# A hybrid decoder step on one core: the input moved ahead of the memory projections, attention keys loaded in 32-channel blocks and transposed by VectorE

## The chip, the core and the metric

The kernel runs on one core of a Trainium2 chip. The metric is the device time of one execution in microseconds (us). TensorE (PE) multiplies, VectorE (DVE) and ScalarE (ACT) do the elementwise work, GpSimd (POOL) does little here, and SyncE (SP) issues most of the DMA transfers. SBUF is the on-chip memory of 128 partitions; PSUM is where PE writes.

## What is computed

One layer of a decoder, for a prompt of 256 tokens and for 8 sample sequences of 4 tokens that share the weights; the two are put side by side as 288 columns. All data are float32.

```python
def mem_kv(mem, g_mem, w_k, w_v):
    m = rms_norm(mem, g_mem)                      # 256 memory tokens x 2048
    k = (m @ w_k).reshape(B, M, X_HEADS, X_HEAD_DIM)   # 4 heads of 512
    v = (m @ w_v).reshape(B, M, X_HEADS, X_HEAD_DIM)
...
def cross_attn(h, k, v, w_q, w_o):
    q = (h @ w_q).reshape(B, S, X_HEADS, X_HEAD_DIM)
    s = einsum('bqhd,bkhd->bhqk', q, k) * (X_HEAD_DIM ** -0.5)
    pr = softmax(s, axis=-1)
    return einsum('bhqk,bkhd->bqhd', pr, v).reshape(B, S, D_MODEL) @ w_o
...
    h = rms_norm(x, g_mix)
    z = h @ w_in                                  # 2048 x 11264: u, v, conv, pool, gates
    ...                                           # three branches, gates, merged
    x = x + merged @ w_out
    x = x + cross_attn(rms_norm(x, g_xattn), mk, mv, w_xq, w_xo)
    x = x + square(relu(rms_norm(x, g_mlp) @ w_up)) @ w_down
```

For the prompt, `mk` and `mv` are `mem_kv` of `mem_prompt` and are outputs too. For the samples they are read from `cache_mem_k` and `cache_mem_v`, 8 batches of 256 tokens by 4 heads by 512 channels: 4 x 512 KB of keys and as much of values for each batch.

## The kernel before, in words

**Weights.** Every product streams its weight matrix from DRAM in chunks of 512 rows by 512 columns (1 MB, four tiles of 128 rows). A list, `plan`, holds the order of the chunks. `load_w` issues a chunk's load on SP's queue into one of three buffers `raw` (L151). `split_w` makes of each half chunk (two tiles, 128 partitions x 1024) a high part on ACT (L165, `w_hi`) and a low part on DVE (L166, `w_lo`); a half is split two halves ahead of its use (`AHEAD`). Activations are split in the same way (`split_act`, `gain_hi`, `gain_lo`, L186 to L193).

**Products.** `proj` keeps the weights stationary and moves 288 columns of activations: for each tile and each of four groups of 128 output channels three matmuls, L232 to L234. `proj_mem`, for the two memory projections, keeps the 256 memory tokens stationary and moves 512 columns of the weights, for each tile and each group of 128 tokens three matmuls, L267 to L269: a half chunk is 12 of them.

**Side work.** `later(n, fn)` puts a function on a list; after each half chunk `tick` runs what is due (in `proj_mem` half a step after each tile). So everything that is not a product is placed by a number of half chunks, and stands in the engines' queues between two products.

**Order before.** The memory rows `mem_prompt` come first (four loads `mem_p`), are transposed by PE (`mem_first`, L348) and projected with `w_xk`, four heads one after the other, while x is loaded (L428 and the line before it), transposed (L434, L435) and normed behind the products. Then `w_in` and the branches, `w_branch`, `w_out`, and `w_xq`. During the last quarter of `w_xq` the memory rows are loaded a second time (`mraw`, L882) and transposed again (`mem_again`), and `w_xv` follows. The samples' attention runs beside `w_xv`: 16 units of 128 memory tokens of a batch, each one 1 MB load of 128 partitions (`k_load`, L901), 16 transposes by PE (L912) that go through PSUM to `kT` by one copy on ACT and one on DVE (L913) for each four, and 16 matmuls of 128 columns (`k_scores`, L921). A unit is due every 0.7 half chunks. `sample_softmax` (L932 to L939), `sample_probs` and 16 units of values (`sample_values`, L969) follow. The prompt's own keys are read back from `k_scr`, head by head (`head_load`, L989), transposed by PE (`head_keys`, L1002) and multiplied (L1011 to L1013, L1032 to L1034). `w_xo` and the MLP end the kernel.

Of the kernel before, what the change touches and what calls it, by code (L numbers as in the profile page):

```python
# [16 lines left out]
P = 128  # L17
# [21 lines left out]
def decoder_step_kernel(  # L39
# [41 lines left out]
    gmem = const.tile([P, 16], F32, name="gmem")  # L81

# [3 lines left out]
    # ---- work that is issued a number of weight steps later, between the products  # L86
# [28 lines left out]
    # ---- operands: weights streamed and split into high and low parts, activations kept split  # L115
# [5 lines left out]
    for h in range(4):  # L121
        planned(w_xk, KT, h * 512)
# [34 lines left out]
    def split_w(i):  # L157
        raw = raws[i // 2]
        t0 = 2 * (i % 2)
        hi = wpool.tile([P, 2, 512], F32R, name="w_hi", tag="w_hi")  # L160
        lo = wpool.tile([P, 2, 512], F32R, name="w_lo", tag="w_lo")
        n = 1 if i == 0 else 2
        for t in range(0, 2, n):
            src = raw[:, t0 + t:t0 + t + n]
            latest["hi"] = s_.copy(hi[:, t:t + n], src)  # L165
            latest["lo"] = v_.tensor_tensor(lo[:, t:t + n], src, hi[:, t:t + n].bitcast(F32), ALU.subtract)  # L166
        halves[i] = (hi, lo)
        if i % 2:
            del raws[i // 2]
# [29 lines left out]
    class Quarters:  # L199
        """Split activations, four channel tiles to a buffer."""  # L200
# [73 lines left out]
    # ---- norms  # L274
# [54 lines left out]
    def rows_rstd(pieces, rows, r_out):  # L329
        ss = small.tile([P, 4], F32, name="ss")  # L330
        n = 0
        for piece in pieces:
            width = min(1024, piece.shape[-1])
            for o in range(0, piece.shape[-1], width):
                junk = actp.tile([P, 1024], F32, name="junk", tag="q_lo3")
                s_.activation(junk[:rows, :width], piece[:rows, o:o + width], AF.Square,
                              accum_out=ss[:rows, n:n + 1])
                n += 1
        ms = small.tile([P, 1], F32, name="ms1")
        v_.reduce_sum(ms[:rows], ss[:rows, :n], axis=AX.X)  # L340
        v_.tensor_scalar(ms[:rows], ms[:rows], 1.0 / DM, RMS_EPS, ALU.mult, ALU.add)
        rpow(r_out, ms[:rows])

    def mem_transposed(nat, m, k2, k0=0):
        pt = psum()
        for d in range(2):
            for c in range(2):
                t_.transpose(pt[:, d * 256 + c * P:d * 256 + (c + 1) * P],  # L348
                             nat[c][:, (k2 - k0 + d) * P:(k2 - k0 + d + 1) * P], ident)
        for part in (gain_hi, gain_lo):  # L350
            for d in range(2):
                part(m.hi(k2 + d), m.lo(k2 + d), pt[:, d * 256:(d + 1) * 256], gmem[:, k2 + d:k2 + d + 1])

    # ------------------------------------------------------------------ branch phase
# [27 lines left out]
    v_.tensor_copy(gmem, vt[:, :16])  # L382
# [5 lines left out]
    later(6, load_vecs)  # L388

    class Halves:  # L390
        def hi(self, kt):
            return mh[kt // 8][:, kt % 8, :]

        def lo(self, kt):
            return ml[kt // 8][:, kt % 8, :]

    mh = [bp.tile([P, 8, MEM], F32R, name=f"mh{i}", tag=("u", "cv")[i]) for i in range(2)]
    ml = [bp.tile([P, 8, MEM], F32R, name=f"ml{i}", tag=("yh", "yl")[i]) for i in range(2)]
    m0 = Halves()

    def mem_first(k2):
        mem_transposed([mem_p[k2 // 4][:, c, :] for c in range(2)], m0, k2, k2 // 4 * 4)
    mem_first(0)
    with tc.issue_after(latest["a_hi"].ins), tc.issue_after(latest["a_lo"].ins):
        advance(0 - AHEAD)
    mem_first(2)
    for i in range(6):
        later(i + 1, lambda i=i: mem_first(4 + 2 * i))
    for c in range(2):
        later(3 + c, lambda c=c: rows_rstd([mp_[:, c, :] for mp_ in mem_p], P, r_mem[:, c:c + 1]))  # L410

    # x: transposed, kept for the residual, normed
    xbox = {}
    x_natp = bp.tile([P, 2, DM], F32, name="x_natp", tag="m")
    xT0 = actp.tile([P, KT, NT], F32, name="xT0", tag="xT")
    r_x = small.tile([P, 3], F32, name="r_x")

    x_nats = []

    def load_x():  # L420
        for c in range(2):
            nc.sync.dma_start(x_natp[:, c, :], x_prompt[0, c * P:(c + 1) * P, :])

    def load_xs():
        xs_ = x_sample.rearrange("b q d -> (b q) d")
        for i in range(2):
            xn = sig([P, 1024], f"x_nats{i}")
# [784 lines left out]
```

## Time and profile before

| what | value |
|---|---|
| time, median of 3 runs | 2191.64 us (2190.96 to 2195.14) |
| span of the profiled execution | 2190.5 us |
| PE busy | 2167.8 us, 99% of the span |
| DVE busy | 1258.6 us, 57% |
| ACT busy | 883.9 us, 40% |
| granted TensorE clock, mean | 0.999 of full speed |
| DMA | 399.63 MB, 182 GB/s over the span |

The runs' times lie around the profiled span; the median is 1.1 us above it. Busy time of PE is modelled from pipelined matmuls, so the distance from one start to the next is the better measure of what an instruction costs there.

### The profile page before, as it was taken

How to read it: one execution, taken by the hardware profiler on the slowest of the kernel's cores; microseconds unless marked ns; L12 is line 12 of the kernel's file. 1: busy time of each engine (PE TensorE's matmuls, PEld its weight loads, DVE VectorE, ACT ScalarE, POOL GpSimd, SP SyncE). 2: the span in 40 equal slices, each digit the busy share in tenths (PEclk: the TensorE clock that was granted, in tenths of full speed). 3: DMA queues.
4: the chain of work that ended last, by engine and by line, in shares of the span. 5: the costliest groups of instructions: out<-in, count | busy, mean ns of one | idle time of the engine just before them, and what ended most of it. 6: DMA issues, size and time to landing. Idle time of an engine off the chain costs nothing.

```text
span 2190.5 us, 37794 instructions
## 1 busy us (share of the span) xinstructions
PE 2167.8 (99%) x16134; PEld 2095.5 (96%) x16134; DVE 1258.6 (57%) x1909; ACT 883.9 (40%) x1200; POOL 27.2 (1%) x72
## 2 busy tenths in 40 slices
PE   8999999999999999999999999999999999999998
PEld 6799999999999999999887799999999999999998
DVE  4656678766775746464555556554455445445554
ACT  6533444333433544343443444333333333333343
POOL 1000000000000000000000000000000000000000
PEclk9999999999999999999999999999999999999999
DMA  8765554455454455444778745555554455555542
GB/s 297 243 202 166 191 176 155 137 172 169 159 173 159 165 203 192 163 165 161 245 277 304 283 164 164 161 167 172 158 171 163 165 170 159 173 162 166 173 155 101
DMA packets 185355, 399.63 MB, mean 182 GB/s; under 512 B 7130, under 2 KB 8778, under 8 KB 180555
## 3 DMA queue, kind: packets, MB, share of 16 engines
q1 hardware_dynamic: 180229, 386.45, 53.3%
q10 hardware_dynamic: 4702, 10.72, 1.3%
q8 instruction: 126, 2.06, 0.4%
q14 instruction: 42, 0.34, 0.0%
q0 software_dynamic: 256, 0.05, 0.0%
HBM read 385.60 MB, written 12.80 MB: 182 GB/s over the span
## 4 chain that ended last, share of the span: by engine, by line
PE 60%; issue 37%; DMA 1%; DVE 1%; ACT 0%; POOL 0%; SPq 0%; POOLq 0%; ACTq 0%; DVEq 0%
PE ps L232 15%; PE ps L234 15%; PE ps L233 15%; PE ps L267 3%; PE ps L268 3%; PE ps L269 3%; PE ps L912 1%; PE ps L921 1%; PE ps L969 1%; DMA kv<-in_cache_mem_v_dram 0%; DMA mem_p<-in_mem_prompt_dram 0%; DMA kv<-in_cache_mem_k_dram 0%; PE ps L683 0%; PE ps L348 0%; PE ps L434 0%
## 5 line engine op out<-in xcount | busy, mean ns | idle before, releaser
L166 DVE TENSOR_TENSOR w_lo<-raw,w_hi 128x1024 fp32r<-128x1024 f32 (+1 forms) x641 | 783.5, 1223 | 821.5 <-ACT w_hi L165 818.7
L165 ACT CAST w_hi<-raw 128x1024 fp32r<-128x1024 f32 (+1 forms) x641 | 670.8, 1047 | 1131.0 <-PE ps L233 987.8
L232 PE MATMUL ps<-q_hi,w_hi 128*128 128x288 f32 x3200 | 945.9, 296 | 0.0
L234 PE MATMUL ps<-q_hi,w_lo 128*128 128x288 f32 x3200 | 943.8, 295 | 0.9 <-DVE w_lo L166 0.9
L233 PE MATMUL ps<-q_lo,w_hi 128*128 128x288 f32 x3200 | 942.2, 294 | 0.0
L232 PEld LDWEIGHTS ps<-q_hi,w_hi 128*128 128x128 f32 x3200 | 600.4, 188 | 1.1
L234 PEld LDWEIGHTS ps<-q_hi,w_lo 128*128 128x128 f32 x3200 | 600.2, 188 | 1.1 <-DVE w_lo L166 1.1
L233 PEld LDWEIGHTS ps<-q_lo,w_hi 128*128 128x128 f32 x3200 | 600.3, 188 | 0.5
L232 PE MATMUL ps<-h_hi,w_hi 128*128 128x288 f32 x1024 | 303.5, 296 | 0.0
L233 PE MATMUL ps<-h_lo,w_hi 128*128 128x288 f32 x1024 | 302.8, 296 | 0.0
L234 PE MATMUL ps<-h_hi,w_lo 128*128 128x288 f32 x1024 | 300.9, 294 | 0.0
L234 PEld LDWEIGHTS ps<-h_hi,w_lo 128*128 128x128 f32 x1024 | 192.6, 188 | 0.0
L233 PEld LDWEIGHTS ps<-h_lo,w_hi 128*128 128x128 f32 x1024 | 192.3, 188 | 0.0
L232 PEld LDWEIGHTS ps<-h_hi,w_hi 128*128 128x128 f32 x1024 | 192.2, 188 | 0.0
L232 PE MATMUL ps<-y_hi,w_hi 128*128 128x288 f32 x384 | 113.6, 296 | 0.0
L233 PE MATMUL ps<-y_lo,w_hi 128*128 128x288 f32 x384 | 113.4, 295 | 0.0
L234 PE MATMUL ps<-y_hi,w_lo 128*128 128x288 f32 x384 | 112.9, 294 | 0.0
L568 DVE SCALAR_TENSOR_TENSOR cv<-glu,cwT,cv 128x256 f32<-128x256 f32 x240 | 105.7, 477 | 0.0
L234 PEld LDWEIGHTS ps<-y_hi,w_lo 128*128 128x128 f32 x384 | 72.2, 188 | 0.0
L232 PEld LDWEIGHTS ps<-y_hi,w_hi 128*128 128x128 f32 x384 | 72.0, 188 | 0.0
L233 PEld LDWEIGHTS ps<-y_lo,w_hi 128*128 128x128 f32 x384 | 72.1, 188 | 0.0
L267 PE MATMUL ps<-w_hi,mh 128*128 128x512 f32 x128 | 52.5, 418 | 0.9 <-ACT w_hi L165 0.9
(305 smaller groups left out, 1437.5 us busy)
## 6 DMA issues: line engine op xcount, KB each, us to landing
raw<-in_w_in_dram SPq DMA_DIRECT2D x88, 1024.0 KB
raw<-in_w_up_dram SPq DMA_DIRECT2D x64, 1024.0 KB
raw<-in_w_down_dram SPq DMA_DIRECT2D x64, 1024.0 KB
raw<-in_w_branch_dram SPq DMA_DIRECT2D x24, 1024.0 KB
raw<-in_w_out_dram SPq DMA_DIRECT2D x16, 1024.0 KB
kv<-in_cache_mem_k_dram SPq DMA_DIRECT2D x16, 1024.0 KB
raw<-in_w_xq_dram SPq DMA_DIRECT2D x16, 1024.0 KB
raw<-in_w_xv_dram SPq DMA_DIRECT2D x16, 1024.0 KB
```

What stands on the lines that cost most here:

```text
L165: latest["hi"] = s_.copy(hi[:, t:t + n], src)
L166: latest["lo"] = v_.tensor_tensor(lo[:, t:t + n], src, hi[:, t:t + n].bitcast(F32), ALU.subtract)
L232: t_.matmul(o, wh, act.hi(kt), start=kt == 0, stop=False)
L233: t_.matmul(o, wh, act.lo(kt), start=False, stop=False)
L234: t_.matmul(o, wl, act.hi(kt), start=False, stop=kt == nkt - 1)
L267: t_.matmul(acc[c], mh, hi[:, i, :], start=kt == 0, stop=False)
L268: t_.matmul(acc[c], mh, lo[:, i, :], start=False, stop=False)
L269: t_.matmul(acc[c], ml, hi[:, i, :], start=False, stop=kt == KT - 1)
L568: v_.scalar_tensor_tensor(o, i, wk, o, ALU.mult, ALU.add)
L912: t_.transpose(pt[:, i * P:(i + 1) * P], kv[:, kt * P:(kt + 1) * P], ident)
L921: t_.matmul(ssc[32 * h:32 * h + 32, c * P:(c + 1) * P], qm[:, 4 * h + k, b, :], kTs[h // 2][:, (h % 2) * 4 + k, :], start=b == 0 and c == ...
L969: t_.matmul(sbox["osc"][32 * h:32 * h + 32, :], sbox["pTm"][:, c, b, h, :], kv[:, h * 512:(h + 1) * 512], start=b == 0 and c == 0, stop=b ...
```

## The change

x and the first chunks of `w_in` are loaded first, with a gain column of their own (`gx`). `x_first` transposes x, splits x times gain without the norm and keeps x; the first group of `w_in` (columns 2048 to 2559) is multiplied with that, and the norm `rb` is applied when its sums leave PSUM. Behind it `x_normed` overwrites the activations with the normed ones for the other groups. The side work of this part is due some seven half chunks later.

`mem_prompt` is loaded once, in the last quarter of `w_xq`, and transposed there; `w_xk` comes between `w_xq` and `w_xv`, its plan entries too. The chunks of `w_xq` are written in a permuted order of columns ("blocked"), in two instructions on each of ACT and DVE for a half chunk where there was one. The keys of a batch come as 16 loads of 32 partitions by 8 pieces of 128 channels (512 bytes each), so that each partition quarter holds the right 32 x 32 blocks; DVE transposes them, four instructions of 128 x 1024 for a batch (`k_transposed`, L914 of the changed kernel), and `k_scores` is 16 matmuls of 256 columns for a batch. A batch is due every 3.8 half chunks over `w_xk`, the values every 3.6 over `w_xv`. `head_load` reads the prompt's keys in four loads of 32 partitions, and `head_keys` transposes on DVE (L1004).

```diff
-    for h in range(4):
-        planned(w_xk, KT, h * 512)
...
-    for w in (w_out, w_xq, w_xv, w_xo):
+    for w in (w_out, w_xq, w_xk, w_xv, w_xo):
...
-        n = 1 if i == 0 else 2
+        blocked = plan[i // 2][0] is w_xq
+        n = 1 if i == 0 or blocked else 2
         for t in range(0, 2, n):
-            src = raw[:, t0 + t:t0 + t + n]
-            latest["hi"] = s_.copy(hi[:, t:t + n], src)
+            dh, dl, src = hi[:, t:t + n], lo[:, t:t + n], raw[:, t0 + t:t0 + t + n]
+            if blocked:
+                dh, dl = (d[:, 0].rearrange("p (b a c) -> p a b c", a=4, b=4) for d in (dh, dl))
+                src = src[:, 0].rearrange("p (a b c) -> p a b c", a=4, b=4)
+            latest["hi"] = s_.copy(dh, src)
...
+    def x_first(kt):
+        pt = psum()
+        cp, o = kt // 4, (kt % 4) * P
+        for c in range(2):
+            t_.transpose(pt[:, c * P:(c + 1) * P], x_p[cp][:, c, o:o + P], ident)
+        t_.transpose(pt[:, NP:NT], x_s[:32, kt * P:(kt + 1) * P], ident[:32, :32])
+        split_act_gain(act.hi(kt), act.lo(kt), pt[:, :NT], gx[:, kt:kt + 1])
+        v_.tensor_copy(x_of(kt), pt[:, :NT])
...
+    def x_normed(kt):
+        hx = t288("hx")
+        v_.scalar_tensor_tensor(hx, x_of(kt), gx[:, kt:kt + 1], xbox["rb"], ALU.mult, ALU.mult)
+        split_act(act.hi(kt), act.lo(kt), hx)
...
+    for i in range(7):
+        for kt in (2 * i + 2, 2 * i + 3):
+            later(max(0.5 * i, 1), lambda kt=kt: x_first(kt))
+    for cp in range(4):
+        later(2 + cp // 2, lambda cp=cp: x_squares(cp))
+    later(4, x_rstd)
+    later(5, lambda: xbox.update(rb=broadcast_tokens(xbox["dg"])))
     for kt in range(KT):
...
+        later(6 + kt // 4 if kt < 8 else 8, lambda kt=kt: x_normed(kt))
...
+            if half == 0:
+                rb = xbox["rb"]
+                v_.tensor_tensor(gp[:, t, 30:286], acc[:, :NP], rb[:, :NP], ALU.mult)
...
-    def k_load(c, b):
-        kv = kv_tile()
-        nc.sync.dma_start(kv, cache_mem_k[0, b, c * P:(c + 1) * P].rearrange("m h d -> m (h d)"))
-        return kv
+    def k_load(b):
+        kvs = []
+        for hp in range(2):
+            kv = kv_tile()
+            for h2 in range(2):
+                for qd in range(4):
+                    nc.sync.dma_start(
+                        kv[32 * qd:32 * qd + 32, h2 * 1024:(h2 + 1) * 1024].rearrange("p (m r) -> p m r", r=P),
+                        cache_mem_k[0, b, :, 2 * hp + h2, qd * P:(qd + 1) * P].rearrange("(m p) r -> p m r", p=32))
+            kvs.append(kv)
+        return kvs
...
+        for h in range(4):
+            kT = split_tile("kT", [P, 4, MEM])
+            v_.transpose(kT.rearrange("p k (m c) -> p k m c", c=32),
+                         kvs[h // 2][:, (h % 2) * 1024:(h % 2 + 1) * 1024].rearrange(
+                             "p (m k r) -> p k m r", k=4, r=32))
...
+                t_.matmul(ssc[32 * h:32 * h + 32, :MEM], qm[:, 4 * h + k, b, :], kTs[h][:, k, :],
+                          start=b == 0 and k == 0, stop=b == NB - 1 and k == 3, tile_position=(0, 32 * h))
...
-    later(12, sample_softmax)
-    later(13, sample_probs)
-    for n in range(16):
-        later(14 + n, lambda n=n: sample_values(v_load(n % 2, n // 2), n % 2, n // 2))
-    later(30, sample_out)
+    for b in range(NB):
+        later(1 + 3.8 * b, lambda b=b: k_unit(b))
+        later(3 + 3.8 * b, lambda b=b: k_scores(kts.pop(b), b))
+        later(33 + 3.6 * b, lambda b=b: v_unit(b))
+    later(31, sample_softmax)
+    later(31.5, sample_probs)
+    later(60, sample_out)
...
+    for h in range(4):
+        def evac_k(c, acc, h=h):
...
+                s_.dma_start(k_scr[c * P:(c + 1) * P, h * 512:(h + 1) * 512], kn)
+                s_.dma_start(new_mem_k[0, 0, c * P:(c + 1) * P, h, :], kn)
+            later(1, put)
+        proj_mem(w_xk, h * 512, m1, evac_k)
```

What SP issues at the start of the samples' attention, before (`kv` are the keys, `raw` the weights, `knat` the prompt's keys):

```order
L151 DMA raw<-in_w_xv_dram 128x4x512
L989 DMA knat<-k_scr 128x2x512
L901 DMA kv<-in_cache_mem_k_dram 128x2048 x2
L151 DMA raw<-in_w_xv_dram 128x4x512
L901 DMA kv<-in_cache_mem_k_dram 128x2048 x3
```

and now:

```order
L154 DMA raw<-in_w_xk_dram 128x4x512
L904 DMA kv<-in_cache_mem_k_dram 32x8x128 x16
L154 DMA raw<-in_w_xk_dram 128x4x512 x2
L904 DMA kv<-in_cache_mem_k_dram 32x8x128 x16
L154 DMA raw<-in_w_xk_dram 128x4x512 x2
```

The same 2 MB of keys for a batch were two transfers and are 16; two weight chunks (one in one place) stand between two batches, and SP keeps to this order.

On DVE, in the same place, before (`kT` are the transposed keys):

```order
L166 TENSOR_TENSOR w_lo<-raw,w_hi 128x1024
L193 SCALAR_TENSOR_TENSOR q_lo_11043<-ps,gmem,q_hi_11042 128x256 x4
L913 COPY kT<-ps 128x512 x2
L166 TENSOR_TENSOR w_lo<-raw,w_hi 128x1024
L913 COPY kT<-ps 128x512 x2
```

and now:

```order
L173 TENSOR_TENSOR w_lo<-raw,w_hi 128x1024 x4
L1070 TENSOR_SCALAR kn<-ps,r_mem 128x512 x2
L914 STREAM_TRANSPOSE kT<-kv 128x1024 x4
L173 TENSOR_TENSOR w_lo<-raw,w_hi 128x1024 x4
L914 STREAM_TRANSPOSE kT<-kv 128x1024 x4
```

The copies out of PSUM are gone; four transposes that wait for the keys' loads stand between the low parts of the weights, which PE needs.

On PE, at the last batch of keys, now (L274 to L276 are the products of `proj_mem`, L923 the scores, L956 the transposes of the samples' probabilities):

```order
L274 MATMUL ps<-w_hi,q_hi_10479 128x512
L275 MATMUL ps<-w_lo,q_hi_10479 128x512
L276 MATMUL ps<-w_hi,q_lo_10480 128x512
L923 MATMUL ps<-kT,qm 32x256 x15
L956 MATMUL ps<-ident,psm 128x128 x2
L274 MATMUL ps<-w_hi,q_hi_10249 128x512
```

The transposes of the probabilities follow the last scores directly, with no product between.

## Rows read from the trace of the kernel before

**Rows 1.** The page: the span, busy time of the engines, and the chain of work that ended last.
```profile
span 2190.5 us, 37794 instructions
PE 2167.8 (99%) x16134; PEld 2095.5 (96%) x16134; DVE 1258.6 (57%) x1909; ACT 883.9 (40%) x1200; POOL 27.2 (1%) x72
PE 60%; issue 37%; DMA 1%; DVE 1%; ACT 0%; POOL 0%; SPq 0%; POOLq 0%; ACTq 0%; DVEq 0%
```

**Rows 2.** The two longest waits of PE for loads of data other than a gain vector, over the whole span: line, what it waited for, us in total, times, longest.
```profile
PE ps L348 <- DMA mem_p<-in_mem_prompt_dram: 2.8, 2, 1.6
PE ps L912 <- DMA kv<-in_cache_mem_k_dram: 1.6, 1, 1.6
```

**Rows 3.** Stretches by time: us, then busy time and instructions of PE, PEld, DVE, ACT, POOL, the granted clock, the share of the 16 DMA engines, GB/s. The first is `w_xk` at the start, the second the middle of the kernel, the third `w_xv` with the samples' attention.
```profile
8.27:116.95 108.68, 106.18 (x463) 83.05 (x464) 67.45 (x105) 62.48 (x108) 2.76 (x5) 1.00 0.80 274
900.00:955.00 55.00, 55.00 (x418) 55.00 (x417) 30.31 (x41) 24.88 (x34) 0.00 (x0) 1.00 0.47 158
1070.16:1251.80 181.64, 179.45 (x1489) 136.82 (x1488) 93.52 (x158) 76.80 (x128) 0.26 (x2) 1.00 0.81 293
```

**Rows 4.** PE's transposes of the samples' keys in the view of their line: count, shortest, median and longest ns, first and last start.
```profile
L912 PE MATMUL ps<-ident,kv x256: 270/273/332, 1068.5 to 1153.9; 128*128 128x128 f32 x128
```

**Rows 5.** PE in order of time where `w_xv` begins: start, us, instruction, count, and the idle time before it with its releaser.
```profile
1066.47 0.29 PE L234 MATMUL ps<-q_hi,w_lo 128*128 128x288 f32 x1
1067.60 1.06 PE L348 MATMUL ps<-ident,mraw 128*128 128x128 f32 x8 [0.83 <-DVE q L891]
1068.50 1.91 PE L912 MATMUL ps<-ident,kv 128*128 128x128 f32 x16
1070.16 0.48 PE L267 MATMUL ps<-w_hi,q_hi 128*128 128x512 f32 x1
...
1073.09 1.08 PE L921 MATMUL ps<-kT,qm 128*32 128x128 f32 x32
...
1075.36 0.39 PE L269 MATMUL ps<-w_hi,q_lo 128*128 128x512 f32 x1
1077.32 1.94 PE L912 MATMUL ps<-ident,kv 128*128 128x128 f32 x16 [1.57 <-DMA kv<-in_cache_mem_k_dram]
```

**Rows 6.** PE in order of time at the start, same columns.
```profile
8.27 1.22 PE L267 MATMUL ps<-w_hi,mh 128*128 128x512 f32 x2 [0.94 <-ACT w_hi L165]
...
13.69 0.63 PE L267 MATMUL ps<-w_hi,mh 128*128 128x512 f32 x1
14.12 0.63 PE L268 MATMUL ps<-w_lo,mh 128*128 128x512 f32 x1
...
18.07 0.39 PE L267 MATMUL ps<-w_hi,mh 128*128 128x512 f32 x1
18.30 0.39 PE L268 MATMUL ps<-w_lo,mh 128*128 128x512 f32 x1
```

**Rows 7.** Groups by line and shape on DVE and ACT: count, busy us, mean ns of one, idle time before them with its releasers.
```profile
L166 DVE TENSOR_TENSOR w_lo<-raw,w_hi 128x1024 fp32r<-128x1024 f32 x639 | 782.2, 1224 | 821.5 <-ACT w_hi L165 818.7 <-PE ps L683 2.1
L193 DVE SCALAR_TENSOR_TENSOR q_lo<-xT,gvec,q_hi 128x288 fp32r<-128x288 f32 x32 | 14.7, 513 | 0.0
L462 DVE TENSOR_SCALAR kn<-ps,r_mem 128x512 f32<-128x512 f32 x8 | 5.8, 746 | 0.9 <-PE ps L269 0.9
L165 ACT CAST w_hi<-raw 128x1024 fp32r<-128x1024 f32 x639 | 669.6, 1048 | 1130.7 <-PE ps L233 987.8 <-PE ps L269 80.2 <-issue 51.7
L190 ACT ACTIVATE q_hi<-xT,gvec 128x288 fp32r<-128x288 f32 x32 | 14.9, 524 | 0.0
L336 ACT ACTIVATE junk<-mem_p 128x512 f32<-128x512 f32 x8 | 5.0, 631 | 0.1
```

**Rows 8.** SP's queue in order of time before `w_xv`: start, us, the transfer issued, count.
```profile
1064.96 0.37 SPq L151 DMA_DIRECT2D raw<-in_w_xv_dram  x1
...
1079.28 0.33 SPq L901 DMA_DIRECT2D kv<-in_cache_mem_k_dram  x1
```

**Rows 9.** Five short stretches, columns as in rows 3: weights in rows of 2048 bytes to 128 partitions; a load in rows of 512 bytes to 128 partitions; the load of x_sample to 32 partitions (rows of 4096 bytes) mixed with weights; the loads of conv states to 120 partitions (rows of 4096 bytes) mixed with weights, and the slowest half microsecond of them.
```profile
34.00:35.00 1.00, 1.00 (x6) 0.81 (x5) 0.93 (x3) 0.91 (x1) 0.00 (x0) 1.00 1.05 401
154.90:156.60 1.70, 1.70 (x15) 1.70 (x15) 0.20 (x1) 1.05 (x1) 0.00 (x0) 1.00 1.03 324
30.50:31.50 1.00, 1.00 (x6) 0.77 (x6) 1.00 (x1) 1.00 (x4) 0.00 (x0) 1.00 0.71 141
49.50:51.50 2.00, 2.00 (x10) 1.64 (x9) 1.09 (x1) 1.97 (x5) 0.00 (x0) 1.00 0.98 206
50.50:51.00 0.50, 0.50 (x4) 0.41 (x3) 0.09 (x1) 0.47 (x2) 0.00 (x0) 1.00 0.88 184
```

**Rows 10.** The samples' softmax in order of time, on DVE: start, us, instruction, and the idle time before it with its releaser.
```profile
1157.49 0.42 DVE L932 TENSOR_REDUCE smax<-ps 128x1 f32<-128x256 f32 x1 [0.96 <-PE ps L921]
...
1161.69 0.34 DVE L939 TENSOR_SCALAR psm<-psm,srec 128x256 f32<-128x256 f32 x1
1161.95 0.15 DVE L934 TENSOR_SCALAR nmax<-smax 128x1 f32<-128x1 f32 x1
...
1162.72 0.17 DVE L938 RECIPROCAL srec<-ssum 128x1 f32<-128x1 f32 x1 [0.63 <-ACT pr L936]
```

**Rows 11.** The same softmax on ACT, same columns.
```profile
1160.12 0.47 ACT L936 ACTIVATE psm<-ps,nmax 128x256 f32<-128x256 f32 x1
1160.49 0.19 ACT L936 ACTIVATION_READ_ACCUMULATOR psm<-ps,nmax 128x1 f32 x1
```

More of the change, by code (lines that the diff above doesn't have):

```diff
@@ L327, in square_acc @@
             v_.tensor_tensor(acc, acc, sq, ALU.add)
[L329 to L352, printed above, removed]
     br = ExitStack()
@@ L387, in load_vecs @@
         v_.tensor_copy(gvec, vt[:, :96])
[L388 to L402, printed above, removed]
@@ L403, in decoder_step_kernel, with x_of @@
-    mem_first(0)
+    later(5, load_vecs)
+    xT0 = [bp.tile([P, 8, NT], F32, name=f"xT0{i}", tag=("yh", "yl")[i]) for i in range(2)]
+    act = Quarters()
+    for _ in range(4):
+        act.add()
+    ss = small.tile([P, 3, 4], F32, name="ss")
+    g_.memset(ss, 1.0)
+    xbox = {}
+    def x_of(kt):
+        return xT0[kt // 8][:, kt % 8, :]
+    def x_first(kt):
[6 more added lines that the diff above has]
+        v_.tensor_copy(x_of(kt), pt[:, :NT])
@@ new lines, in x_squares, with x_rstd @@
+    def x_squares(cp):
+        for c in range(3):
+            piece = x_p[cp][:, c, :] if c < 2 else x_s[:32, cp * 512:(cp + 1) * 512]
+            rn = P if c < 2 else 32
+            junk = small.tile([P, 512], F32, name="junk", tag="kn", bufs=3)
+            s_.activation(junk[:rn], piece, AF.Square, accum_out=ss[:rn, c, cp:cp + 1])
+    def x_rstd():
+        ms = small.tile([P, 3], F32, name="ms")
+        v_.reduce_sum(ms, ss, axis=AX.X)
+        v_.tensor_scalar(ms, ms, 1.0 / DM, RMS_EPS, ALU.mult, ALU.add)
+        r = small.tile([P, 3], F32, name="r_tok")
+        rpow(r, ms)
+        xbox["dg"] = token_diag(r)
@@ L413, in decoder_step_kernel @@
[L413 to L427, printed above, removed]
-            nc.sync.dma_start(xn[:32], xs_[:, i * 1024:(i + 1) * 1024])
-            x_nats.append(xn)
@@ L431, in x_transposed @@
-    def x_transposed(kt):
-        pt = psum()
-        for c in range(2):
-            t_.transpose(pt[:, c * P:(c + 1) * P], x_natp[:, c, kt * P:(kt + 1) * P], ident)
-        t_.transpose(pt[:, NP:NT], x_nats[kt // 8][:32, (kt % 8) * P:(kt % 8 + 1) * P], ident[:32, :32])
-        s_.copy(xT0[:, kt, :], pt[:, :NT])
-    act = Quarters()
-    def x_normed(kt):
-        if kt % 4 == 0:
-            act.add()
-        hx = t288("hx")
-        v_.scalar_tensor_tensor(hx, xT0[:, kt, :], gcol(G_MIX, kt), xbox["rb"], ALU.mult, ALU.mult)
-        split_act(act.hi(kt), act.lo(kt), hx)
@@ L457, in decoder_step_kernel @@
-    later(21, lambda: s_.dma_start(x_scr, xT0))
-    for h in range(4):
-        def evac_k(c, acc, h=h):
-            kn = small.tile([P, 512], F32, name="kn", bufs=3)
-            v_.tensor_scalar(kn, acc, r_mem[:, c:c + 1], None, ALU.mult)
-            def put():
-                s_.dma_start(new_mem_k[0, 0, c * P:(c + 1) * P, h, :], kn)
-                s_.dma_start(k_scr[c * P:(c + 1) * P, h * 512:(h + 1) * 512], kn)
-            later(1, put)
-        proj_mem(w_xk, h * 512, m0, evac_k)
-    while len(act.t) < 4 or any(e[0] < clock[0] + 1 for e in pending):
-        tick()
+    x_first(1)
@@ L878, in decoder_step_kernel @@
     mbox = {}
+    mss = small.tile([P, 2, 4], F32, name="mss")
     def mem_load(qr):
@@ L926, in decoder_step_kernel @@
+    mem_transposed(3)
+    mem_rstd()
     for b in range(NB):
```

168 lines of the change are left out of this document (90 added, 78 removed).

## The prediction, made before the changed kernel had run

> **What bounds the kernel now.** I read the page first, then PE's waits, then the stretches by stage, then the order of time at the places the change touches. PE is busy for 99% of the span, and the chain that ended last is PE and its issue [rows 1]. The two longest waits for data are 2.8 and 1.6 us [rows 2]. In the middle of the kernel PE starts 418 matmuls of 288 columns in 55 us, 0.132 us each, while DVE is busy 30.3 us and the DMA engines 0.47 of the time [rows 3]. So the time is a sum of PE's work, and a change pays only by taking work from PE or waits from its queue. It costs where another resource takes over, and two stages are near that: `w_xk` at the start (DMA share 0.80, DVE 67 of 109 us) and `w_xv` with the samples' attention (0.81, 94 of 182 us) [rows 3]. The change reworks both.
>
> **PE work removed.** 16 transposes of keys start at 1068.50 and the next product at 1070.16 [rows 5], 0.104 us each. Gone are the 256 of the keys [rows 4], 32 of the prompt's keys (four heads, eight each) and 32 of the memory rows, which were transposed twice: 320 x 0.104 = 33.3 us. The copies out of PSUM go with them; DVE and ACT had idle time, so those count nothing. The scores become half as many matmuls of twice the columns; 16 of 128 columns take 1.08 us [rows 5], so a batch took 2.1 us and I take 2.0 to 2.1 now: 0.7 us gained at most, taken as 0.7. Two gaps of that stage go: 0.83 us before the last memory transposes, and 1.57 us for the second unit of keys [rows 5]. Sum -36.4.
>
> **Start.** x takes the place of the memory rows, with the same transposes (48 of x, whenever they run), so the bulk is neutral: the first product waits for a 512 KB load and the first half chunk either way, at 8.27 us before [rows 6]. Cold clock also remains: the step from one 512-column product to the next is 0.43 us at 13.69 and 0.23 us at 18.07 [rows 6], the lower and the higher of its two levels. New is how closely DVE and ACT must follow. The first `w_in` group is 16 x 4 x 3 = 192 matmuls, 25.3 us at 0.132. In it ACT does 16 splits of x at 0.524, 12 squares at 0.631 (plus some 0.19 to read the sum, [rows 7, 11]) and 8 high parts at 1.048: 8.4 + 9.9 + 8.4 = 26.7 us. DVE does 16 low parts at 0.513, 16 copies of x at some 0.46 and 8 low parts at 1.224: 25.4 us [rows 7]. Three engines that must each work 25 us in lockstep end late: worked through by hand with these durations, the first group ends near 48 us instead of 41, and the second waits once more, some 6 us, because `x_normed` puts 16 products with the norm and 16 low parts in front of a low part of the weights on DVE. Against it stand the waits and cold steps that the old start had in the same place, 108.7 us less 384 x 0.233 = 89.5 and some 12 of transposes, 7 us [rows 3, 6]. I take +4, from -2 (x as smooth as the memory rows) to +11 (all of the new 11 us on top of a start no shorter).
>
> **Keys.** This decides. Per batch PE has 3.8 half chunks of 12 products at 0.233 (10.6 us) and 2 us of scores, 12.6 us. In that time the DMA engines must bring 2 MB of keys and, by the order on SP, 13 weight chunks between the first and the last batch, and write 1 MB for each of three heads. A chunk of 1 MB at 401 GB/s [rows 9] is 2.6 us: 34 + 8 = 42 us beside the keys. With k us for a batch the last keys have been moved 8k + 42 us after the first began. The first can begin only behind its neighbours: a chunk of `w_xv` was issued 5.2 us ahead of the first product [rows 5, 8], so I put the first packet of keys half a microsecond before the first product of `w_xk`; landing and the last two transposes add 2 and 2.4 us. PE gets to the last scores after 31.33 half chunks x 2.8 + 7 x 2.05 = 102 us. So PE waits about 8k + 46 - 102 = 8k - 56, and nothing if that is negative.
>
> What is k? Rows of 512 bytes to 128 partitions moved at 324 GB/s with the engines full [rows 9]: 2.10 MB in 6.5 us, k = 6.5, and no wait. But the keys go to 32 partitions at a time, and transfers to fewer than 128 partitions are slow in this trace: the load of x_sample fell to 141 GB/s with the engines at 0.71, that is 199 at full share; the states' 120 partitions to 206 at 0.98, in its worst part 184 [rows 9]. At 184 k = 11.4 and the wait 35 us. I take 210 (206 by its share), k = 10.0 and a wait of 24 us, because the 32-partition row lies on that side and not near 324; its own scaled 199 gives 28.
>
> [...]
>
> DVE in a batch's 12.6 us: four transposes, 3.8 low parts at 1.224 and half a pair of `kn` at 0.746. No row has a transpose; the nearest is the low part of the same 128 x 1024 shape. At 1.224, DVE needs 4.9 + 4.7 + 0.8 = 10.4 us, so it keeps up; at twice that, 15.3, it would not, 8 x 2.7 = 22 us by itself, hidden by the wait for DMA at k = 10. At half it changes nothing. SP's issues, 16 x 0.33 [rows 8] = 5.3 us, are covered by the batch.
>
> **The rest.** The samples' softmax now stands between the last scores and the transposes on PE, with nothing between: reduce 0.42, 0.15, exponential 0.47 + 0.19, reciprocal 0.17, scale 0.34 [rows 10, 11], 1.7 us; I take +1.5, 0 to +2.5. `w_xq`'s split in two pieces and the squares of the memory rows lie beside products of 288 columns, where DVE and ACT have nearly half their time free; cover gone, 32 half chunks x some 0.2 us. The values are spread over all of `w_xv`: 0, from -2 to +3. The memory rows' second load is saved, 2 MB on an engine that isn't full there: 0.
>
> **Sum.** 2190.5 - 36.4 + 4 + 24 + 1.5 = 2183.6 us against the profiled span; the median of the runs is 1.1 above that span, so **2184.5 us**. With the wait for keys from 13 to 31 us (k from 8.6 to 10.9) the forecast's own range is 2173 to 2192.
>
> **Rivals.**
> A. *The keys move at the 324 GB/s rate.* [...] Against: the x_sample load. No wait for keys: 2183.6 - 24 = 2159.6, by the runs 2160.5.
> B. *The two key buffers close a loop, and the kernel gets slower.* A batch fills both `kv` tiles, so a batch's first load can't be issued until DVE has transposed the first tile before it, and SP, in order, holds the weight chunks behind it. A batch then costs its transfer (10 us), 2 us to land, two transposes with the low parts in front of them (up to 4.9) and an issue (0.4 to 0.6): 17.4 us instead of 15 of pure DMA. 8 x 17.4 + 5 - 102 = 42 us of waiting: 2201.6, by the runs 2202.7. It decides from a wait of 35 us on, a batch of 16.5 us. For: DVE's queue puts the transposes between low parts whose weights come behind the keys. Against: two chunks between batches give the engines 5 us of other work, about what landing and transposing take.
> C. *The start loses all it can.* +11 instead of +4: 2191.5 by the runs, no measurable change. For: lockstep of three engines. Against: the old start also had its waits.
>
> **Chances.** A measurement of this kernel tells 0.2% from nothing, 4.4 us: faster is below 2187.3, slower above 2196.0. The forecast with the milder part of C: 0.52; A: 0.24; B (or the 184 GB/s end with a bad start): 0.22; others 0.02. Of the forecast's share about 0.37 is below 2187.3, 0.14 between. Faster 0.61, same 0.17, slower 0.22. The range 2156 to 2204 takes A with a gain at its ends (smooth start), the forecast, and B at its price.
>
> **What would show it.** Transposes by PE gone but for 48 of x, 32 of the memory rows and the small ones; the step of products unchanged at 0.132 and 0.233. In `w_xk` a stretch of some 125 us where PE waits for weights or scores 24 us in all, with the DMA share near 1 and 200 to 250 GB/s; under A the share lies below 0.9 with 270 GB/s or more; under B the share is clearly below 1 while DVE or SP waits, and the stage takes over 140 us. A transpose on DVE near 1.2 us. At the start, two waits on `w_lo` of a few microseconds each and the second `w_in` group late. Wrong would be: waits elsewhere than these two stages, or `w_xv` no shorter than its 181.6 us [rows 3].

## The result: slightly slower, and where the time is

The changed kernel takes 2198.5 us in the median of 9 runs (2193.6 to 2202.3) against 2191.4 before (2190.8 to 2195.1). The ratio is 1.0027, with a 95% interval of 1.0017 to 1.0037: slower. The forecast was 2184.5, faster, with 2156 to 2204 as its range. The time lies in the range, on the wrong side of no change. The runs of the changed kernel also spread more, 8.8 us.

The page of the changed kernel's profiled run (2195.65 us), in the columns of [rows 1]:

```profile
span 2193.9 us, 36832 instructions
PE 2147.2 (98%) x15559; PEld 2059.9 (94%) x15559; DVE 1289.0 (59%) x1972; ACT 863.6 (39%) x1188; POOL 25.3 (1%) x70
...
PE 54%; issue 38%; DMA 5%; DVE 1%; SPq 1%; ACT 0%; ACTq 0%; POOL 0%; POOLq 0%; DVEq 0%
```

PE is busy for 20.6 us less, as intended, but the span is 3.4 us longer. DMA is now 5% of the chain where it was 1%: PE's work has been exchanged for waiting. PE's waits over the span name the place, as [rows 2] did before:

```profile
PE ps L923 <- DVE kT L914: 16.3, 13, 2.2
PE ps L956 <- DVE psm L941: 5.4, 1, 5.4
PE ps L365 <- DMA gm_n<-in_g_mix_dram: 3.7, 1, 3.7
PE ps L275 <- DVE w_lo L173: 3.1, 6, 0.5
```

The scores wait for the transposed keys and the probabilities for the softmax. The list counts only matmuls that themselves waited. The weight loads (LDWEIGHTS) ahead of them on PE's second queue waited too, 23.4 us in 15 pieces for the same keys, so more comes out of the stage's length. The stretches below are `w_xk` and `w_xv` of the changed kernel, then a stretch in which only keys move, one with weights, one more with keys, and the time from the first packet of keys to the last (columns of [rows 3]):

```profile
973.21:1124.11 150.90, 123.82 (x646) 81.72 (x644) 87.28 (x84) 36.68 (x41) 2.66 (x9) 0.97 1.07 266
1124.11:1255.87 131.76, 131.76 (x703) 97.49 (x701) 73.61 (x127) 57.43 (x95) 0.00 (x0) 0.98 0.77 271
1000.00:1003.00 3.00, 3.00 (x15) 2.49 (x14) 3.00 (x5) 0.00 (x0) 0.00 (x0) 1.00 1.22 200
1005.00:1009.00 4.00, 2.53 (x22) 1.31 (x24) 2.20 (x2) 0.00 (x0) 0.00 (x0) 1.00 1.05 369
1020.00:1023.00 3.00, 3.00 (x14) 2.46 (x14) 1.56 (x2) 0.00 (x0) 0.00 (x0) 1.00 1.19 195
974.24:1110.24 136.00, 117.33 (x606) 78.91 (x605) 75.86 (x71) 30.77 (x32) 1.63 (x7) 0.99 1.08 253
```

`w_xk` takes 150.9 us, of which its 384 products at 0.2275 are 87.4. The DMA share is above 1 for the whole stage (1.07), and where keys move the engines are full (1.19 to 1.22) at 195 to 200 GB/s. That is the rate of the 32-partition row scaled up, 199 [rows 9]; a part of that row's bytes were weights, so the agreement is partly chance. The key packets run from 974.2 to 1110.2, 136 us. Set against 8k + 42, that makes k = 11.75 us for a batch, with all that the 42 us leave out counted in it.

Against before, by stage of the two profiled runs: the part up to the 1000th product of `w_in`, without the 89.6 us of `w_xk`'s products, is 5.6 us shorter; from there to the end of `w_xq` both need some 811.2 us; the gap behind it is 1.7 us shorter; `w_xk` and `w_xv` together take 282.7 us, where before it was 181.64 [rows 3] + 89.6 = 271.2, so 11.4 longer; the rest is 0.6 shorter. The sum is +3.4, the difference of the spans.

### The profile page after: what moved, and what is told of

Same layout as the page of the kernel before. It is cut to its first block, busy times and chain, and to the rows that moved or that the text cites. A ratio compares the mean times of both kernels' runs of the same rounds, so it can differ in the third digit from the quotient of the medians.

```text
span 2193.9 us, 36832 instructions
## 1 busy us (share of the span) xinstructions
PE 2147.2 (98%) x15559; PEld 2059.9 (94%) x15559; DVE 1289.0 (59%) x1972; ACT 863.6 (39%) x1188; POOL 25.3 (1%) x70
## 4 chain that ended last, share of the span: by engine, by line
PE 54%; issue 38%; DMA 5%; DVE 1%; SPq 1%; ACT 0%; ACTq 0%; POOL 0%; POOLq 0%; DVEq 0%
PE ps L239 15%; PE ps L241 15%; PE ps L240 15%; DMA kv<-in_cache_mem_k_dram 2%; DMA raw<-in_w_xk_dram 2%; PE ps L275 2%; PE ps L274 2%; PE ps L276 2%; PE ps L971 1%; DMA k_scr<-kn 1%; DVE w_lo L173 0%; DMA raw<-in_w_in_dram 0%; SPq L904 0%; PE ps L647 0%; DMA out_dram<-kn 0%
## 5 line engine op out<-in xcount | busy, mean ns | idle before, releaser
L275 PE MATMUL ps<-w_lo,q_hi 128*128 128x512 f32 x256 | 102.8, 401 | 3.1 <-DVE w_lo L173 3.1
L274 PE MATMUL ps<-w_hi,q_hi 128*128 128x512 f32 x256 | 101.9, 404 | 1.7 <-ACT w_hi L172 1.7
L276 PE MATMUL ps<-w_hi,q_lo 128*128 128x512 f32 x256 | 101.1, 395 | 0.0
```

Source lines behind the costliest of these rows:

```text
L274: t_.matmul(acc[c], mh, hi[:, i, :], start=kt == 0, stop=False)
L275: t_.matmul(acc[c], mh, lo[:, i, :], start=False, stop=False)
L276: t_.matmul(acc[c], ml, hi[:, i, :], start=False, stop=kt == KT - 1)
```

## The experiments

Two theories stood for the wait of 38 us or more. **Rate**: transfers to 32 partitions are slow. **Loop**: the two key buffers and the transposes' place on DVE set the pace (rival B).

### Key transfers to 128 partitions

```diff
-                        kv[32 * qd:32 * qd + 32, h2 * 1024:(h2 + 1) * 1024].rearrange("p (m r) -> p m r", r=P),
-                        cache_mem_k[0, b, :, 2 * hp + h2, qd * P:(qd + 1) * P].rearrange("(m p) r -> p m r", p=32))
+                        kv[:, h2 * 1024 + qd * 256:h2 * 1024 + (qd + 1) * 256].rearrange("p (m r) -> p m r", r=P),
+                        cache_mem_k[0, b, :, 2 * hp + h2, qd * P:(qd + 1) * P].rearrange("(m p) r -> p m r", p=P))
```

> The changed kernel with the same 16 key transfers per batch, the same 128 KB each and the same 512-byte pieces, but each transfer goes to 128 partitions (2 pieces in each) instead of 32 (8 pieces in each). The keys land in other places than the scores need, so the sample scores are not those of the reference; all work and all bytes are there. Theory rate (transfers to 32 partitions move at some 180 GB/s, 11.8 us for a batch): packets go from 45 to 27 ns, a batch from 11.8 to 6.5 or 7 us, the wait of PE for keys from 41 us to 0 to 5: 2156 to 2163 us. Theory loop (the two buffers and the place of the transposes on DVE set the pace): a batch can't get below transfer 6.5 + landing 2 + two transposes behind low parts 4.9 + issue 0.5 = 13.9 us against PE's 12.6, 10 us or more of waiting stay and the packets' speed matters little: 2167 us or more.

Measured: 2181.4 us, ratio 0.9955 (0.9938 to 0.9971). Its `w_xk`, the time from the first packet of keys to the last, and a stretch with keys alone:

```profile
974.47:1110.88 136.41, 123.73 (x646) 80.15 (x644) 86.11 (x84) 37.19 (x42) 2.75 (x9) 0.99 0.93 296
975.47:1095.69 120.22, 114.73 (x590) 74.78 (x589) 76.25 (x72) 31.31 (x33) 1.75 (x7) 1.00 0.92 283
1013.00:1018.00 5.00, 5.00 (x22) 3.24 (x21) 3.31 (x3) 1.30 (x2) 0.00 (x0) 1.00 0.88 253
```

Same bytes, same pieces, same number of transfers: only the partitions differ, and the keys move at 253 GB/s with the engines no longer full (0.88), packets at 27 ns in place of 45 (medians). From the first key to the last it is 120.2 us for 136.0, and the stage is 14.5 us shorter. So the rate of transfers to 32 partitions is a cause. But 2181 is above the rate theory's 2156 to 2163, by some 20 us, and inside what the loop theory left open (2167 or more): this run alone does not exclude the loop. A part of the 20 us can be read from SP's issues of keys, here and in the changed kernel (count, shortest, median and longest ns):

```profile
L904 SPq DMA_DIRECT2D kv<-in_cache_mem_k_dram x128: 367/467/2780, 971.7 to 1093.2; - x128
L904 SPq DMA_DIRECT2D kv<-in_cache_mem_k_dram x128: 311/442/1970, 970.4 to 1106.0; - x128
```

At 0.47 us and some 0.05 between two, 128 KB come at some 255 GB/s, so the 253 match the pace of SP's issues: 8.2 us for a batch and not the 6.5 of the rate theory.

### Buffers of one head

```diff
-        kv = xp.tile([P, DM], F32, name="kv", bufs=2)
+        kv = xp.tile([P, DM // 2], F32, name="kv", bufs=4)
...
```

> The changed kernel with four buffers of one head (128 x 1024) in place of two of two heads, for keys and values, same memory: a buffer comes free one transpose earlier and the next batch's first load can be issued 1.3 to 3 us sooner. Transfers, bytes and partitions as in the change; values come as twice as many loads of half the size. Theory loop: the pace of a batch falls by 1.3 us or more, 10 us or more in all: 2187 us or less. Theory rate: the engines are held by slow packets, not by the buffers: 2193 to 2199 us.

Measured: 2213.4 us, ratio 1.0100 (1.0085 to 1.0115). `w_xk`:

```profile
972.70:1125.70 153.00, 128.42 (x645) 84.19 (x644) 87.25 (x84) 36.87 (x42) 2.76 (x9) 0.92 1.05 264
```

Earlier free buffers didn't shorten the stage (153.0 us for 150.9). The loss lies behind it: `w_xv` took 148.1 us for 131.8, where the values now came in twice as many loads. The waits of SP's queue in the changed kernel, from 965 to 1125 us, say the same of the buffers:

```profile
SPq L904 <- DMA raw<-in_w_xk_dram: 30.5, 13, 4.2
SPq L904 <- DMA kv<-in_cache_mem_k_dram: 21.1, 39, 4.1
...
SPq L904 <- DMA k_scr<-kn: 5.0, 5, 1.5
...
SPq L904 <- DVE kT L914: 2.2, 1, 2.2
```

Issues of keys waited for transfers ahead of them to land, and once, 2.2 us, for a transpose that frees a buffer. The loop theory falls for `w_xk`; what the halved value loads cost wasn't studied further.

### 128 partitions, keys in their places

One transfer for each 32 tokens of a head, 32 for a batch.

```diff
-                for qd in range(4):
+                for m in range(8):
...
+                    nc.sync.dma_start(
+                        kv[:, h2 * 1024 + m * P:h2 * 1024 + (m + 1) * P],
+                        cache_mem_k[0, b, m * 32:(m + 1) * 32, 2 * hp + h2, :].rearrange("p (q r) -> q p r", q=4))
```

> The changed kernel with the keys in their right places, but each transfer goes to 128 partitions: 32 rows of tokens, four quarters of 128 channels, one 512-byte piece in each partition, 64 KB; so 32 transfers for a batch instead of 16. Theory rate: 27 ns packets as in the run with 128 partitions, unless SP, which needs 0.33 to 0.46 us for an issue, 10.6 to 14.7 us for a batch, becomes the bound: 2157 to 2180 us, 2160 if the issues are hidden. Theory loop: 2167 us or more, as little better as the run with 128 partitions.

Measured: 2309.9 us, ratio 1.054. PE waited 105.4 us in 30 pieces for `kT`. Three microseconds in the middle of a batch:

```profile
1009.00:1012.00 3.00, 3.00 (x12) 2.17 (x11) 2.57 (x3) 1.05 (x1) 0.00 (x0) 0.79 0.29 84
```

The same view of SP's issues as in the first run:

```profile
L904 SPq DMA_DIRECT2D kv<-in_cache_mem_k_dram x256: 521/722/3421, 970.4 to 1222.6; - x128
```

The engines stand at 0.29. An issue of this shape held SP for 0.72 us in the median, so 64 KB each came at 84 GB/s: SP was the bound. The expectation took 0.33 to 0.46 us for an issue, which was too little. Two things had not been kept apart. In the changed kernel an issue of 128 KB took 0.31 us where SP had stood idle and some 0.45 directly behind another one, with some 0.05 between, 7.9 us a batch; the 0.33 us of [rows 8] is an issue that stood alone. And for these 64 KB the same two figures are 0.52 and 0.72. The run says nothing on rate or loop.

### Keys transposed by PE

`k_load`, `k_transposed`, `k_scores`, `head_load` and `head_keys` as before, `w_xq` not permuted, a unit every 1.9 half chunks over `w_xk`.

```diff
-        later(1 + 3.8 * b, lambda b=b: k_unit(b))
-        later(3 + 3.8 * b, lambda b=b: k_scores(kts.pop(b), b))
+        for n in (2 * b, 2 * b + 1):
+            later(1 + 1.9 * n, lambda n=n: k_unit_t(n))
+            later(2 + 1.9 * n, lambda n=n: k_unit_s(n))
```

> The changed kernel with the key part undone: keys in 16 loads of 1 MB to 128 partitions, transposed by PE and copied out of PSUM as before, one unit every 1.9 half chunks over w_xk; the prompt's keys as before; w_xq not permuted. The start, the single load of the memory rows, the place of w_xk, the values over w_xv stay. Both theories: PE's work grows by 288 transposes, 30 us, the 41 us of waiting for keys go, of the softmax wait of 5.4 some 4 go: 2197 + 30.6 - 41 - 4 = 2183 us, 2178 to 2187; if the start had cost what was predicted (4 us) rather than gained 2, it would be 2189.

Measured: 2184.8 us (8 runs), ratio 0.9970 (0.9960 to 0.9981). This is the rest of the change without its key part, and it is faster than before. It puts a size on the key part: with it the time rises to 2198.5. `w_xk` is 139.7 us with some 27 us of transposes in it (256 at 0.104).

### Scores in one piece

In the change one score matmul is issued when its head is ready, products follow, and 15 come later. In the run with 128 partitions a batch's pieces took 3 x 0.55 + 1.84 us and an estimated 0.1 us at each change of kind (in the changed kernel the product at 1108.53 us, behind scores, is followed after 0.34 us, where the step is 0.23), some 3.85 us; 2.0 to 2.1 had been predicted.

```diff
-            for h in range(4):
+            for h in (3, 2, 1, 0):
```

> The changed kernel with one edit: the scores of a batch begin with the head that is transposed last, so that their 16 matmuls stand together on PE instead of one or two of them between products and the rest later. If the scores' own time on PE counted in the change (3.85 us a batch where broken up, 2.1 in one piece), the stage would fall by some 12 us: 2185. If the slow key packets set the pace of each batch, PE only waits longer in the same place: 2193 to 2198.

Measured: 2200.0 us, ratio 1.0037 (1.0023 to 1.0052), no better than the change and above both expected numbers. The wait, now in one piece, has a price of its own. Three of the eight batches, and then a wait and the scores behind it as stretches, and the scores of the middle one, with the granted clock in the column before the last two:

```profile
1010.61 1.93 PE L923 MATMUL ps<-kT,qm 128*32 128x256 f32 x32 [2.31 <-DVE kT L914]
...
1047.05 3.59 PE L923 MATMUL ps<-kT,qm 128*32 128x256 f32 x32 [2.34 <-DVE kT L914]
...
1066.32 3.64 PE L923 MATMUL ps<-kT,qm 128*32 128x256 f32 x32 [4.56 <-DVE kT L914]
```

```profile
1061.00:1066.00 5.00, 0.76 (x4) 0.30 (x2) 2.31 (x2) 0.00 (x0) 0.00 (x0) 0.81 1.13 269
1066.30:1069.90 3.60, 3.58 (x33) 1.57 (x33) 0.85 (x1) 1.93 (x2) 0.00 (x0) 0.50 1.21 219
1047.05:1050.50 3.45, 3.45 (x32) 1.58 (x32) 1.23 (x1) 1.32 (x2) 0.00 (x0) 0.51 1.11 304
```

After 4.56 us of idleness the scores take 3.64 us, at a granted clock of 0.50, where the first batch shown takes 1.93 us after 2.31. Six of the eight batches ran at that clock. One of them had waited 2.34 us, hardly longer than the batch that kept the full clock, so the length of the wait alone does not tell which. Six times some 1.5 us are 9 us, near the 12 us that whole scores were to give: whether the pieces cost anything by themselves stays open.

### Probabilities later

```diff
-        later(33 + 3.6 * b, lambda b=b: v_unit(b))
+        later(37 + 3.2 * b, lambda b=b: v_unit(b))
...
-    later(31.5, sample_probs)
+    later(36, sample_probs)
```

> The changed kernel with the transposes of the samples' probabilities due at step 36 instead of 31.5, so that products of w_xv stand between them and the last scores, and the values at 37 + 3.2 b. PE's wait of 5.4 us for the softmax should go: 2191 to 2193 us, 4 to 6 less than the change; if the wait only moves to the first products of w_xv, whose weights come behind the last keys, 2195 to 2198.

Measured: 2192.1 us (10 runs), ratio 1.0007 (0.9998 to 1.0016). The wait at the probabilities is gone from the list, `w_xk` is 147.0 us for 150.9. With these two due times the change would have measured as no change instead of slower. The changed kernel's DVE rows say why the wait was 5.4 us and not the 1.7 of the chain's operations:

```profile
1118.40 0.42 DVE L934 TENSOR_REDUCE smax<-ps 128x1 f32<-128x256 f32 x1 [2.07 <-PE ps L923]
1119.20 1.76 DVE L949 MEMSET pTm<- 128x2048 f32 x1 [0.38 <-issue]
1120.88 0.10 DVE L936 TENSOR_SCALAR nmax<-smax 128x1 f32<-128x1 f32 x1
1120.90 2.35 DVE L173 TENSOR_TENSOR w_lo<-raw,w_hi 128x1024 fp32r<-128x1024 f32 x2
1123.16 0.16 DVE L940 RECIPROCAL srec<-ssum 128x1 f32<-128x1 f32 x1
```

A memset of 1.76 us and two low parts of the weights stand on DVE between the softmax's steps.

### 128 partitions, whole scores, late probabilities

The first run's transfers with the two edits above.

> The run with key transfers to 128 partitions (2181.4 us, keys in other places than the scores need), with whole scores and late probabilities added. [...] If the 25 us that were missing there are waits for keys or weights, it stays above 2172.

Measured: 2173.9 us, ratio 0.9922 (0.9907 to 0.9937). The 25 us are the first run's 2181.4 less the 2156 of the rate theory. The two edits had been put at an estimated 20 us: 8 x 1.7 = 13 for the scores (3.85 us a batch less some 2.1) and 7 for the softmax's wait, 7.2 in the first run's trace. Of these 20 us 7.5 came. Most of the rest stands as waits for weights, 10.1 us for `w_lo` where the run without the edits had 0.8. SP's queue in one such place, and the stretch in it:

```profile
1005.96 7.41 SPq L904 DMA_DIRECT2D kv<-in_cache_mem_k_dram  x6
```

```profile
1010.50:1012.00 1.50, 1.50 (x9) 1.12 (x8) 1.50 (x2) 1.30 (x2) 0.00 (x0) 1.00 0.19 71
```

Six issues of keys take SP 7.4 us while the DMA engines fall to 0.19, and the weights are behind them on the queue. What SP's queue waited for from 1004 to 1020 us:

```profile
SPq L904 <- DMA k_scr<-kn: 4.6, 1, 4.6
SPq L904 <- DMA raw<-in_w_xk_dram: 3.6, 1, 3.6
SPq L904 <- DVE kT L914: 0.3, 1, 0.3
```

So it was not a buffer (0.3 us), but transfers that had to land. In the trace's records the loads of keys and weights and the writes of the prompt's keys share eight semaphores, which count landings, and an issue waits until the transfer that used its semaphore before has landed: the issue at 1010.95 us waits for that of a write to `k_scr` (256 KB, on ACT's queue at 1006.12), which has landed at 1010.93. In the changed kernel, in the same way, the issue at 1015.18 us waits for a write to `k_scr` issued at 1009.61 and landed at 1015.16. The first run has the same wait, 10.1 us in two pieces. No run moves the writes or changes the sharing, so what this costs in time wasn't measured.

### Keys spread over both stages

With whole scores, the softmax due at 42 and the probabilities at 43.5.

```diff
-        later(1 + 3.8 * b, lambda b=b: k_unit(b))
+        later(1 + 5.4 * b, lambda b=b: k_unit(b))
...
-        later(33 + 3.6 * b, lambda b=b: v_unit(b))
+        later(44.5 + 2.15 * b, lambda b=b: v_unit(b))
```

> The changed kernel with whole scores, right data, and the keys spread: a batch every 5.4 half chunks over w_xk and a part of w_xv, softmax at 42, the values every 2.15 half chunks behind it. DMA work of both stages as the change's run shows it: keys 8 x 11.8 = 94, values 42, weights 32 x 2.65 = 85, writes 16, the prompt's keys 12: 249 us, where the change takes 282.7 for both stages. So at best 30 us less; PE's work there is some 235. With waits for latency left I expect 10 to 22 us less than the change, 2175 to 2187. If the pace of a batch is set by a loop of buffers and not by the engines, the loop takes its 17 us only where PE has 17.2, and the same 2175 to 2187 would come from that; the waits of PE in w_xv would then be the smaller part.

Measured: 2187.8 us (10 runs, 2182.9 to 2192.7), ratio 0.9985 (0.9975 to 0.9995), just above what was expected. Both stages take 274.3 us for 282.7, in the profiled run, which was the slowest of the ten. PE still waited 15.5 us for keys, in five pieces of up to 4.3, and 10.5 us for weights. Both theories had given the same number, so the run does not choose between them.

### The partition quarters in another order

```diff
-                for qd in range(4):
+                for qd in (0, 2, 1, 3):
```

> The changed kernel with the four key transfers of a head issued for the partition quarters 0, 2, 1, 3 instead of 0, 1, 2, 3; nothing else. If neighbouring transfers in flight share what their partitions reach, and quarters 0 and 2 reach different halves, the 512-byte packets fall from 45 ns towards 27, a batch from 11.8 to some 8 us, and PE's wait by 8 x 3.8 = 30 us at most, 17 to 25 with the other limits that the 128-partition run showed: 2172 to 2183. If each transfer is held by its own 32 partitions, whatever runs beside it, packets stay at 44 to 46 ns: 2194 to 2199 us. [...]

Measured: 2193.5 us (10 runs), ratio 1.0017 (1.0005 to 1.0028). `w_xk`, and keys alone:

```profile
973.37:1118.68 145.31, 123.59 (x645) 82.60 (x644) 86.53 (x84) 36.62 (x41) 2.49 (x9) 0.95 1.01 276
994.00:1000.00 6.00, 6.00 (x28) 4.94 (x27) 4.00 (x6) 2.10 (x2) 0.00 (x0) 1.00 1.21 241
```

Packets take 35 ns (median over the stage) for 45, keys alone move at 241 GB/s for 200, and the stage is 5.6 us shorter. A whole batch gains less, since weights are mixed in; the eighth, in the changed kernel and here:

```profile
1098.40:1110.20 11.80, 11.27 (x48) 8.60 (x48) 5.63 (x6) 2.48 (x3) 0.00 (x0) 1.00 1.20 214
1093.60:1104.70 11.10, 11.10 (x52) 7.78 (x44) 5.97 (x5) 3.15 (x4) 0.00 (x0) 0.95 1.03 230
```

Neither of the expected numbers came. The halves in the expectation were the author's assumption, which no run shows; this one shows what the order does. What runs beside a transfer matters, and not only its own 32 partitions, but the packets do not get down to the 27 ns of 128 partitions. The time itself is not clearly better than the change's: the two intervals overlap, and the profiled run was the fastest of the ten.

### Two batches ahead, and both

The first batch is loaded and transposed and the second loaded during the last two quarters of `w_xq`, where the DMA engines are half idle (share 0.50 from 915 to 966 us in the changed kernel); six follow every 5 half chunks.

```diff
+        if h == 2:
+            later(2, lambda: k_early(0, 0))
+            later(5, lambda: k_early(0, 1))
+            later(8.5, lambda: k_early_t(0))
+            later(10, lambda: k_early(1, 0))
+            later(13, lambda: k_early(1, 1))
...
```

> The changed kernel with right data and two batches of keys fetched ahead: the first is loaded and transposed, the second loaded, during the last two quarters of w_xq, where the DMA engines are busy half of the time; the other six follow every 5 half chunks, softmax at 34.5, probabilities at 37, values at 38 + 2.93 b. If the transfer time of the keys (11.8 us a batch) bounds the stage, 2 x 11.8 = 24 us leave it, and with the softmax wait gone (5 us, as in the run with late probabilities, 2192) it is 2168 to 2178. If the pace of each batch were set otherwise (by a loop of buffers), the wider spacing alone would give what f4_spread gave, 2183 to 2190.

> The run with two batches ahead, with the quarters in the order 0, 2, 1, 3. If the order makes the packets shorter, 2160 to 2168; if not, the same as the run with two batches ahead within 2 us.

Measured: 2180.1 us, ratio 0.9951 (0.9936 to 0.9965), and with the order 0, 2, 1, 3 2174.4 us, ratio 0.9932 (0.9916 to 0.9948), both a little above what was expected, the first below the 2183 to 2190 of a loop. The second beats both kernels and the run with PE's transposes (2184.8): DVE's transposes pay once the transfers have room. The intervals of the two overlap, so what the order adds is not clear of noise. The longest waits of the second for data:

```profile
PE ps L860 <- DMA mraw<-in_mem_prompt_dram: 5.0, 2, 3.0
PE ps L274 <- ACT w_hi L172: 3.9, 1, 3.9
...
PE ps L937 <- DVE kT L904: 3.1, 3, 1.4
```

The keys cost 3.1 us there; the memory rows, now behind early keys on SP's queue, 5.0.

> The run with the keys transposed by PE (2184.8) with the probabilities due at 35 and the values at 36 + 3.3 b. Its softmax wait was 1.6 us: 2182 to 2185. It is the version without slow key transfers and without DVE transposes; if the early loads of the run before it beat this one, the transposes by DVE are worth keeping once the transfers are hidden.

Measured: 2185.2 us (7 runs), ratio 0.9973 (0.9962 to 0.9984): no different from 2184.8.

## Why the prediction was wrong

**What bounds the kernel**: right, PE's work, with `w_xk` and `w_xv` near other limits. **PE work removed** (-36.4): right in kind. The 256 + 32 + 32 transposes are gone, and PE is busy 20.6 us less, with stretches at a low clock in that (0.50 from 1121.5 to 1128.3 us). With the measured terms below in the sum, -36.4 - 2.3 + 38 + 5.9 = +5.2 us, against +3.4 measured, so the size was about right too.

**Start** (+4): wrong in sign. It gained 5.6 us, 3.3 of them memory transposes that the first term already has, so it stands at -2.3. The lockstep was there, the first group ends at 46.3 us where 48 was worked out, and the second took 29.1 us for 25.3, a wait of 3.8 and not 6. The two steps of 512-column products go with the clock: in the changed kernel it is 0.43 us from 1124.68, where the granted clock is 0.50, and 0.23 us from 1069.09, where it is 1.00. At the start of the kernel before, the first record of a clock, 1.00, begins at 17.2 us, where the step falls to 0.23; the level ahead of it is inferred from the step.

**Keys** (+24): this is the step that failed. The sum put the transfers from the first key to the last at 8 x 10 + 42 = 122 us; they took 136. The rest of the formula held to some 3 us: 136 + 4 - 102 is a wait of 38, and 87.4 of products, 16.4 of scores, 38 and the softmax's 5.9 make 147.7 of the 150.9 us of `w_xk`. The 2 us to land in that 4, and in rival B's batch, no run shows: in the changed kernel's trace the last packet of keys ends at 1110.24 us and its transfer has landed at 1111.43, 1.2 us later. The run with 128 partitions shows the partitions to be the reason for the slow packets: with it the 136 us became 120.

Of the 14 us, 4 are the rate: the 16.8 MB of keys take 84 us at the 200 GB/s that the engines moved with keys alone (10.5 us a batch) and 80 at the 210 that was taken. 10.0 was read from a stretch where states went to 120 partitions and scaled up, although the row of the same 32 partitions lay below it; both rows were mixed with weights, and weights alone moved at 401. Another 2 us are bytes: at 253 GB/s over 136 us, 17.6 MB moved beside the keys, 44 us at 401 and not 42. The last 8 lie in the changes between keys, weights and writes and weren't taken apart, so 11.75 is the price of a batch with these changes, above even the upper end of 11.4. With k = 10.5 the forecast would have been some 2189, still not slower.

**DVE**: a transpose of 128 x 1024 was taken at 1.224 us from the nearest row; it is this:

```profile
L914 DVE STREAM_TRANSPOSE kT<-kv 128x1024 f32<-128x1024 f32 x32 | 39.2, 1236 | 21.7 <-DMA kv<-in_cache_mem_k_dram 20.3 <-issue 1.3
```

DVE stood idle for 20.3 us before them because of keys that had not landed, and did not bind.

**The rest** (+1.5 for the softmax): 5.9 us from the start of the last score to the probabilities, 4.4 more. The operations were counted, but not what stood between them on DVE. Keys 14 and softmax 4.4 too small, the start 6 too large: 12 us, near the 10.3 between the predicted 2183.6 and the profiled span. (2183.6 + 1.1 is 2184.7, not 2184.5, and rival A's 2159.6 is 2160.7 by the runs.)

**Rivals.** A (2160.5) is refuted, and beyond its rate too: keys moved at 200 GB/s, and with fast packets the time was 2181. The 324 GB/s row was not of 512-byte rows alone: in the trace's packets of that stretch they carry 153 of the 324, and the rest came in pieces of 2 KB. B named the size (42 us of waiting, 2202.7 us), by a mechanism that didn't hold: buffers that come free sooner did not shorten the stage, and SP waited 2.2 us for one. Of the signs set for B a stage over 140 us came, a DMA share clearly below 1 did not (1.07). That the range holds the time is owed to B's price at its upper end, so it is luck. C did not occur.

## What to carry to other kernels

A layout that saves an engine's work can be paid for by the transfers that feed it: before moving work from a full engine, sum the transfers of the stage at the rate of a row with the same number of partitions, and place them where the DMA engines are idle. Set beside it the pace of the queue that issues them, read from issues that follow one another closely: 16 to 32 small transfers for a batch came near it or over it here. When a chain of short steps is moved to a place where PE has nothing between its ends, count what stands between the steps on the other engines' queues, not the steps alone. A first run that differs only in the suspected property, even with data in the wrong place, says more than one that mends it and changes the number of issues too.

## What was not expected of the hardware

The order of the quarters alone raised the rate of 32-partition transfers from 200 to 241 GB/s in stretches with keys alone, and from 214 to 230 in the eighth batch with some weights in it. Six of eight score batches behind a wait ran at half the clock (0.50 and 0.51 granted in the two shown), one of them after 2.34 us of idleness, 3.59 us for 1.93. An issue on SP took 0.31 us for 128 KB in 256 pieces when SP had stood idle and some 0.45 directly behind another one, and 0.52 and 0.72 for 64 KB in 128 pieces of a transposed order; 0.33 had been read for 1 MB in two dimensions, standing alone [rows 8].
